# A gated two-branch decoder step: late subtractions of low parts, staged LayerNorm chunks, mixing between a pair's outputs

## The chip, the cores and the metric

One core of a Trainium2 chip runs the whole step in one program. The metric is device time in microseconds, the median of the runs; the profile is one further execution of the same program. TensorE multiplies matrices, VectorE and ScalarE work element by element, GpSimd and SyncE mostly issue transfers here.

## The reference

```python
h = rmsnorm(x, norm_g)
z = jnp.einsum('btd,de->bte', h, w_in)                 # 7 groups of 1024 columns
a_val, a_gate, a_silu, p_in, p_silu, g_a, g_b = jnp.split(z, idx, axis=-1)
u = a_val * jax.nn.sigmoid(a_gate)
c, new_conv = causal_depthwise_conv(u, buf_conv, conv_w, conv_b)      # width 31
c = jax.nn.silu(layernorm(c, ln_g, ln_b)) * jax.nn.silu(a_silu)
br_a = jnp.einsum('btc,cd->btd', c, w_conv_out)
pooled, new_pool = multiscale_pool(p_in, buf_pool, start_pos)         # means over 2, 4, 8, 16
q = jnp.einsum('btgc,gce->btge', pg, w_pool_mix).reshape(B_, T_, D_POOL)   # 4 groups of 256
q = q * pool_scale * jax.nn.silu(p_silu)
br_b = jnp.einsum('btc,cd->btd', q, w_pool_out)
merged = jax.nn.sigmoid(g_a) * br_a + jax.nn.sigmoid(g_b) * br_b
y = rmsnorm(x + jnp.einsum('btd,de->bte', merged, w_out), final_g)
```

16 learned tokens and 1024 prompt positions run with zero states, and 8 samples of 8 positions with given states. Outputs are y of both and the new states.

## The kernel before, in words

Channels lie on the 128 partitions and the 1104 positions on the free axis, in two halves h (552 each; 544 without the learned tokens, H2). A 1024-channel tensor is 8 chunks (NK). Products of fp32 precision are made from two fp32r parts: a high part (a cast on ScalarE) and a low part (source minus high part); each chunk costs three matmuls (high x high, high x low, low x high) in two column units (`gemm`, L150). The low part comes in two ways: `split` (L119) subtracts on VectorE behind the cast; `split_dma` (L124) writes minus the high part on ScalarE and adds the source by a DMA that GpSimd issues. PSUM is four buffers of two banks (`bank2`).

Order of the work: the plain outputs p0 to p5, then the plain `blocks` g0 v0 p6 p7 g1 v1 (a half output is 48 matmuls), then 22 pairs of outputs (`ORDER`: g, v, q, b, a, s). A pair makes two outputs with seven half-depth products of 24 matmuls each (`seven`, L456) out of sums of operands (`make_t`, L751, the T operands) and sums of weights (`Weights`). Products of neighbouring pairs are interleaved: q2, b, q1 of a pair, a of the next, q4, d, q3 of the next. `prepare(t)` loads a weight 8 products ahead, sums it 5 and splits it 4 ahead. Between the pairs that follow q0 to q3, `Mix` (L805) multiplies the pooled tensor by its 256 x 256 group matrices in four parts (12 matmuls each) and gates each (`gate`, L845). Then come the 8 pool outputs `ppo` (loop at L1013), the LayerNorm of the convolved tensor, the 8 conv outputs `pco` (loop at L1078, the first two made chunk by chunk in four PSUM buffers), and the last projection `pwo`.

Every engine runs its instructions in the order in which the program issues them; slots, banks and half buffers are given out in that order too (34 slots, 10 weight halves, 6 weight operands, 11 half buffers). What sets the place of VectorE's free-standing work, above all the 240 taps of the convolution (L677) and the pooling, is a planner: `todo` is a queue of (cost, work); `step(us)` advances a planned TensorE clock and runs what `defer` has put off by so many steps; `spend(n)` charges VectorE's planned clock with 0.22 + n/960 us; `fill(until)` issues work from `todo` as long as that clock is under TensorE's plus 1.5:

```python
    def fill(until=None):
        while todo and (until is None or clock["dve"] < until + LAG):
```

LayerNorm of the convolution goes over all channels, so it needs sums over the 8 chunks: `sum_rest` (L964) adds the chunks that were not stored, `begin_totals` (L970) splits the sum and defers by one step the 8 matmuls with a matrix of ones (`total_products`, L194), `centre` (L979) subtracts the mean and squares, a second `begin_totals` gives the variance, `root` (L987) the inverse root, and `branch_a` (L992) scales a chunk, applies Silu, multiplies by the silu path and splits it into the operand cx. In the `ppo` loop a step is a whole half output (6 planned us), and the fill is left out for output 0.

Of the kernel before, what the change touches and what calls it, by code (L numbers as in the profile page):

```python
# [69 lines left out]
def hybrid_trunk_kernel(  # L70
# [116 lines left out]
    def total_products(hl, n, name):  # L187
        out = slot(f"total_{name}", (2, n))
        for half in range(2):
            ps = bank2(f"pt{half}_{name}")  # L190
            for u in range(2):
                c = slice(u * n // 2, (u + 1) * n // 2)
                for i in range(2):
                    pe.matmul(ps[:, u, : n // 2], ones, hl[i][:, half, c], start=(i == 0), stop=(i == 1))  # L194
# [212 lines left out]
    class Weights:  # L407
# [19 lines left out]
        def split(self, what):  # L427
            o = op_tile(f"wo{what}_{self.name}", (2, NQ, P))
            if what in ON_DVE:
                split(o[:, 0], o[:, 1], self.raw[what])  # L430
                spend(512)
# [16 lines left out]
    def product(out, w, t, units, first, last):  # L448
        prepare(clock["t"])
        gemm(out, lambda k, s: w[:, s, k], lambda k, s: t[k][:, s], units, tuple(range(NQ)), first, last)  # L450
        clock["t"] += 1
        step(T_PRODUCT)

    def seven(w, units, put):  # L456
# [3 lines left out]
        def product_of(out, what, t, first, last):  # L460
            product(out, w.op.pop(what), t_ops[t], units, first, last)
# [16 lines left out]
        product_of(x, "q2", "T2", False, False)  # L478
        c2 = keep("c2")
# [4 lines left out]
        product_of(x, "q1", "T1", False, False)  # L484
        c4 = keep("c4")
# [319 lines left out]
    class Mix:  # L805
# [13 lines left out]
        def split_w(self):  # L819
            self.w = op_tile(f"m{self.g}", (2, 2, 2 * P))  # L820
            split(self.w[:, 0], self.w[:, 1], self.wraw.rearrange("p (k a) c -> p k (a c)", k=2))
            spend(512)
            del self.wraw

        def split(self, h):
            for k in range(2):
                self.x[k, h] = operand(f"px{2 * self.g + k}{h}", self.raw.pop((k, h)), split)
                spend(H2)
# [25 lines left out]
    for n, (kind, i) in enumerate(blocks):  # L854
        left = len(blocks) - n
        if n + 2 < len(blocks):
            ops[n + 2].load()
        if n + 1 < len(blocks):
            ops[n + 1].split(split)
            spend(512, 2)  # L860
        if left in (3, 2):
            make_t(3 - left, split_dma)
        if left == 1:
            for t in range(-LEAD_LOAD, -LEAD_SPLIT):
                prepare(t)
        for h in (0, 1) if left > 1 else (1, 0):
            ps = bank2(f"p{kind}{i}{h}")
            gemm(ps, ops[n], lambda k, s: hx[h][k][:, s], UNITS1, every, True, True)
            step(2 * T_PRODUCT)
            if kind == "v":  # L870
                fill(clock["pe"])
            put_block(kind, i, h, ps[:, :, : HT // 2])
            if left == 1:
                for t in (-4, -3) if h else (-2, -1):
                    prepare(t)
                if h:
                    make_t(2, split)
                    make_t(3, split)
            if left > 1:
                fill(clock["pe"])  # L880
        if kind == "p":
            push(pool_work(i), soon=False)
        if kind == "v":
            defer(1, lambda i=i: Conv(i))
    clock["t"] = 0
# [14 lines left out]
    mix = None  # L900
    for n in range(len(pairs)):
        nxt = pairs[n + 1][1] if n + 1 < len(pairs) else iter(())
        if mix:
            mix.split(0)
            mix.split_w()
            mix.load(1)
# [17 lines left out]
        if mix:  # L924
            mix.gate(*mix.part(1, 0))
# [4 lines left out]
        else:  # L930
            coming = None
# [28 lines left out]
    def load_sum():  # L960
        norm["sum"] = slot("lcsum", (2, H2))
        sp.dma_start(out=norm["sum"], in_=csum[0])
# [305 lines left out]
```

## Time and profile before

| | |
|---|---|
| median of 3 runs | 1029.25 us (1027.83 to 1029.61) |
| profiled execution | 1030.44 us, span 1028.7 us |
| TensorE matmul busy | 956.8 us, 93%, 7032 instructions, mean granted clock 0.964 |
| VectorE busy | 774.1 us, 75% |
| ScalarE busy | 478.6 us, 47% |
| GpSimd busy | 177.1 us, 17% |
| DMA | 187.08 MB, mean 182 GB/s |

Busy is the time in which an engine had an instruction running. A matmul counts as busy also at a low granted clock. The granted clock is a share of TensorE's 2.4 GHz; 0.5 is its lower level of 1.2 GHz. An engine that idles costs nothing unless the chain that ends last runs over it.

### The profile page before, as it was taken

To read this page: it belongs to the slowest core of one execution; us is meant where nothing else is said; L and a number is where in the kernel's file an instruction comes from. 1 tells how busy PE (TensorE), PEld (TensorE's weight loads), DVE (VectorE), ACT (ScalarE), POOL (GpSimd) and SP (SyncE) were. 2 spreads that over 40 slices of the span, in tenths; PEclk is the share of its full clock that TensorE was granted. 3 is DMA by queue.
4 is the path that set the end of the run, shared out by engine and by line. 5 is a ranking of instruction groups with operands and counts; after the bars stand their busy time and mean duration, and the time that the engine had idled before them with its cause. 6 is when DMAs were issued, how large, how long until landed. Compare 5 with 4: busy or idle time off the path is not lost.

```text
span 1028.7 us, 17986 instructions
## 1 busy us (share of the span) xinstructions
PE 956.8 (93%) x7032; PEld 930.3 (90%) x7032; DVE 774.1 (75%) x1011; ACT 478.6 (47%) x793; POOL 177.1 (17%) x216
## 2 busy tenths in 40 slices
PE   9999997999999999999999999899980779999995
PEld 9999996999999899999999999899980669998884
DVE  6569987978898878889999999669965565464343
ACT  7644345544555545555656565641145542234111
POOL 0001322322232122222232323022110100000000
PEclk9999998999999999999999999999995689999998
DMA  9323795798797876978989787997753665432222
GB/s 320 109 89 122 249 252 129 153 225 203 168 210 173 206 196 160 243 186 218 227 195 226 194 213 174 298 335 194 200 148 134 142 166 184 139 115 110 94 71 103
DMA packets 104358, 187.08 MB, mean 182 GB/s; under 512 B 21840, under 2 KB 25296, under 8 KB 104272
## 3 DMA queue, kind: packets, MB, share of 16 engines
q1 hardware_dynamic: 70720, 121.98, 37.0%
q0 software_dynamic: 24336, 46.05, 25.9%
q10 hardware_dynamic: 9216, 17.90, 4.6%
q8 instruction: 55, 0.90, 0.3%
q14 instruction: 31, 0.25, 0.1%
HBM read 93.92 MB, written 48.71 MB: 139 GB/s over the span
## 4 chain that ended last, share of the span: by engine, by line
PE 74%; DVE 11%; ACT 6%; DMA 5%; issue 3%; SPq 1%; DVEq 0%; ACTq 0%; POOLq 0%; POOL 0%
PE pp L150 9%; PE ppo L150 8%; PE pco L150 8%; PE px_b L150 5%; PE px_a L150 5%; PE pwo L1141 4%; PE px_s L150 4%; PE px_q L150 4%; PE px_v L150 4%; PE px_g L150 3%; DVE c L677 3%; PE pg L150 2%; PE pv_a L150 2%; PE pv_v L150 2%; DMA xr<-in_xres 2%
## 5 line engine op out<-in xcount | busy, mean ns | idle before, releaser
L677 DVE SCALAR_TENSOR_TENSOR c<-ce,pv,c 128x1024 f32<-128x1024 f32 x240 | 308.1, 1284 | 5.8 <-ACT c L654 1.2
L150 PE MATMUL pco<-cx,w_co 128*128 128x272 f32 x768 | 110.2, 308 | 28.3 <-ACT cx L120 14.2
L150 PEld LDWEIGHTS pco<-cx,w_co 128*128 128x128 f32 x768 | 106.9, 206 | 31.7 <-ACT cx L120 14.9
L150 PE MATMUL ppo<-q,w_po 128*128 128x272 f32 x768 | 97.0, 288 | 1.3 <-ACT w_po L120 0.9
L150 PEld LDWEIGHTS ppo<-q,w_po 128*128 128x128 f32 x768 | 96.5, 188 | 1.7 <-ACT w_po L120 1.1
L1141 PE MATMUL pwo<-wo,mx 128*128 128x512 f32 x336 | 79.2, 394 | 0.0
L1141 PEld LDWEIGHTS pwo<-wo,mx 128*128 128x128 f32 x336 | 63.1, 188 | 14.7
L150 PE MATMUL pp<-xg,wh_p 128*128 128x276 f32 x384 | 65.6, 291 | 0.4 <-DVE xg L219 0.3
L150 PEld LDWEIGHTS pp<-xg,wh_p 128*128 128x128 f32 x384 | 55.0, 189 | 1.3 <-ACT xg L218 0.7
L1160 DVE TENSOR_TENSOR xr<-pwo,xr 128x1024 f32<-128x1024 f32 (+1 forms) x9 | 10.0, 1106 | 41.2 <-PE pwo L1141 20.6
L150 PE MATMUL pp<-xg,wl_p 128*128 128x276 f32 x192 | 40.0, 290 | 0.0
L120 ACT CAST mx<-lga 128x544 fp32r<-128x544 f32 x16 | 10.3, 647 | 61.9 <-DVE lga L1102 61.9
L1123 ACT ACTIVATE sq<-xr 128x1024 f32<-128x1024 f32 (+1 forms) x9 | 8.7, 964 | 65.2 <-DVE xr L1160 65.2
L150 PE MATMUL px_q<-tT,woq_q 128*128 128x272 f32 x192 | 28.5, 310 | 4.5 <-ACT py_q L475 4.5
L150 PEld LDWEIGHTS px_q<-tT,woq_q 128*128 128x128 f32 x192 | 27.5, 210 | 4.9 <-ACT py_q L475 4.9
L125 ACT CAST w_po<-raw_po 128x512 fp32r<-128x512 f32 x14 | 8.6, 612 | 49.5 <-DMA raw_po<-in_w_po 49.1
L150 PEld LDWEIGHTS pp<-xg,wl_p 128*128 128x128 f32 x192 | 30.3, 188 | 0.0
L1101 DVE TENSOR_TENSOR lga<-pco,lga 128x544 f32<-128x544 f32 x16 | 11.6, 723 | 24.6 <-PE pco L150 24.6
L150 PE MATMUL px_b<-tT,woq_b 128*128 128x272 f32 x192 | 25.5, 289 | 2.3 <-ACT py_b L475 2.3
L150 PE MATMUL pmix<-px,m 128*128 128x272 f32 x192 | 27.1, 289 | 0.5 <-DVE zq L845 0.5
L150 PE MATMUL px_s<-tT,woq_s 128*128 128x272 f32 x192 | 25.4, 288 | 2.0 <-ACT c_s L465 2.0
L150 PEld LDWEIGHTS px_b<-tT,woq_b 128*128 128x128 f32 x192 | 24.5, 188 | 2.8 <-ACT py_b L475 2.8
(412 smaller groups left out, 2220.1 us busy)
## 6 DMA issues: line engine op xcount, KB each, us to landing
lraw<-d_raw SPq DMA_DIRECT2D x16, 276.0 KB, 3.4
d_pool<-pool SPq DMA_DIRECT2D x8, 544.0 KB, 4.5
lp<-d_pool SPq DMA_DIRECT2D x16, 272.0 KB, 4.8
lq<-d_q SPq DMA_DIRECT2D x16, 272.0 KB, 5.5
lb<-d_sgb SPq DMA_DIRECT2D x16, 272.0 KB, 4.6
d_tb<-lb SPq DMA_DIRECT2D x16, 272.0 KB, 2.5
lsa<-d_sa SPq DMA_DIRECT2D x16, 272.0 KB, 4.7
ltb<-d_tb SPq DMA_DIRECT2D x16, 272.0 KB, 3.3
```

Source lines behind the costliest of these rows:

```text
L120: act.copy(dst_h, src)
L125: act.copy(dst_h, src)
L150: pe.matmul(out[:, u, : hi - lo], w(k, a), xs(k, b)[:, lo:hi], start=first and k == ks[0] and i == 0, stop=last and k == ks[-1] and i == 2 ...
L677: dve.scalar_tensor_tensor(c, s, wk, c, ALU.mult, ALU.add)
L1101: dve.tensor_tensor(of_half(ga), ps, of_half(ga), ALU.mult)
L1123: act.activation(sq[:rows, c], xr[:, c], AF.Square, accum_out=a1 if ns[0] else a0)
L1141: pe.matmul(ps[:, n - ns[0]], x(k), wo[k][n][w], start=(k == 0 and s == 0), stop=(k == NK - 1 and s == len(passes) - 1),)
L1160: dve.tensor_tensor(v3(xr[:, c], 512), ps[:, : len(ns)], v3(xr[:, c], 512), ALU.add)
```

## The change

- `split_late` casts at once and defers the subtraction by one step. It replaces `split` for the weight q4 of each pair, for Mix's matrix and inputs, and for q chunks 0 to 5; for q 6 and 7 `split` stays and its subtractions are no longer charged to the planner.
- In `seven`, the copies c2 and c4 are issued before the step's deferred work instead of behind it, and there is one more place to pause, between product b with its output and product q1.
- Mix's part (0,0) comes before q1, its gate and part (0,1) between q1 and the next pair's a; parts (1,0) and (1,1) together between q4 and d, with their gates behind both. Its first loads are issued before the next pair's a, and its first splits behind d.
- The last two plain blocks run g1 h1, v1 h1, g1 h0, v1 h0, with `make_t(0)` to `make_t(3)` and the preparations spread between them, and fill only in v1.
- In the pool outputs a step is half a half output (3 planned us); output 0 is filled too; the stored chunks are loaded in output 0 and the sum in output 1, where the summing also enters `todo`. The mean's and variance's matmuls can so come between half products. (`begin_totals` and `total_products` take lists; each is called with one sum, as before.)
- `branch_a` is staged: the scaling and Silu of chunk i+1 are issued before chunk i's multiplication, and the subtractions of a chunk behind the next but one's scaling; its planned cost is 4.2 instead of 5.2.

```diff
+    def split_late(dst_h, dst_l, src):
+        act.copy(dst_h, src)
+        spend(src.free_size())
+        defer(1, lambda: dve.tensor_tensor(dst_l, src, dst_h.bitcast(F32), ALU.subtract))
...
-    def product(out, w, t, units, first, last):
+    def product(out, w, t, units, first, last, then):
         prepare(clock["t"])
         gemm(out, lambda k, s: w[:, s, k], lambda k, s: t[k][:, s], units, tuple(range(NQ)), first, last)
         clock["t"] += 1
+        kept = then and then()
         step(T_PRODUCT)
+        return kept
...
-        product_of(x, "q2", "T2", False, False)
-        c2 = keep("c2")
+        c2 = product_of(x, "q2", "T2", False, False, lambda: keep("c2"))
         fill(clock["pe"])
         product_of(y, "b", "21", False, True)
         fill(clock["pe"])
         put(0, 0, y[:, :, :n])
-        product_of(x, "q1", "T1", False, False)
-        c4 = keep("c4")
+        yield
+        c4 = product_of(x, "q1", "T1", False, False, lambda: keep("c4"))
...
+    ops[nb - 1].split(split)
+    spend(512, 2)
+    make_t(0, split_dma)
+    plain_half(nb - 2, 1)
+    for t in range(-LEAD_LOAD, -LEAD_SPLIT):
+        prepare(t)
+    make_t(1, split_dma)
+    plain_half(nb - 1, 1)
+    make_t(2, split)
+    prepare(-4)
+    plain_half(nb - 2, 0)
+    make_t(3, split)
+    for t in (-3, -2):
+        prepare(t)
+    plain_half(nb - 1, 0)
+    prepare(-1)
+    defer(1, lambda: Conv(blocks[-1][1]))
...
-        q.append([operand(f"q{j}{h}", z, split) for h, z in enumerate(qraw.pop(j))])
-        spend(H2, 2)
+        q.append([operand(f"q{j}{h}", z, split if j > 5 else split_late) for h, z in enumerate(qraw.pop(j))])
...
         next(cur)
         if mix:
-            mix.gate(*mix.part(0, 0))
-        next(nxt, None)
+            tail = mix.part(0, 0)
+        next(cur)
         if mix:
+            mix.gate(*tail)
             mix.gate(*mix.part(0, 1))
             mix.split(1)
-        next(cur)
-        if mix:
-            mix.gate(*mix.part(1, 0))
         if 0 <= n - first_q < 4:
             coming = Mix(n - first_q)
             coming.load(0)
             coming.load_w()
-        else:
-            coming = None
+        next(nxt, None)
+        next(cur)
+        if mix:
+            tails = [mix.part(1, 0), mix.part(1, 1)]
+            for tail in tails:
+                mix.gate(*tail)
...
         next(cur)
-        tail = mix.part(1, 1) if mix else None
+        if coming:
+            coming.split(0)
+            coming.split_w()
+            coming.load(1)
         next(nxt, None)
-        if tail:
-            mix.gate(*tail)
         next(nxt, None)
-        mix = coming
+        mix, coming = coming, None
...
+    def scale(i):
+        if i < NK:
+            dve.tensor_tensor(conv[i], conv[i], norm["rstd"], ALU.mult)
+            act.activation(conv[i], conv[i], AF.Silu, bias=col(OFF_LB, i), scale=col(OFF_LG, i))
...
     def branch_a(i):
+        scale(i + 1)
+        while low:
+            low.popleft()()
+        if i == NK:
+            return
         load_sa(i + 2)
         cx.append([])
...
-            cx[i].append(operand(f"cx{i}{h}", conv[i][:, h], split_dma if i in (1, 3, 5) else split))
+            if i in (1, 3, 5):
+                cx[i].append(operand(f"cx{i}{h}", src, split_dma))
+            else:
+                o = slot(f"cx{i}{h}", (2, H2), F32R)
+                act.copy(o[:, 0], src)
+                low.append(
+                    lambda o=o, src=src: dve.tensor_tensor(o[:, 1], src, o[:, 0].bitcast(F32), ALU.subtract)
+                )
+                cx[i].append(o)
...
-            ps = gemm_half(f"ppo{d}", po[d], q, h, NK)
-            step(2 * T_PRODUCT)
-            if d < 2:
-                load_conv(d * 4 + h * 2, d * 4 + h * 2 + 2)
-            if d == 2 and h == 0:
+            ps = bank2(f"ppo{d}{h}")
+            for ks in (range(NQ), range(NQ, NK)):
+                gemm(ps, po[d], lambda k, s: q[k][h][:, s], UNITS3, tuple(ks), ks[0] == 0, ks[0] > 0)
+                step(T_PRODUCT)
+                if ks[0] == 0 and d > 0:
+                    fill(clock["pe"])
+            ps = ps[:, :, : H2 // 2]
+            if d == 0:
+                load_conv(h * 4, h * 4 + 4)
+            if d == 1 and h == 0:
                 load_sum()
...
-            if d > 0:
-                fill(clock["pe"])
+            fill(clock["pe"])
```

## Rows read from the trace of the kernel before

**Rows 1.** Page, the chain that ended last, shares of the span by engine

```profile
PE 74%; DVE 11%; ACT 6%; DMA 5%; issue 3%; SPq 1%; DVEq 0%; ACTq 0%; POOLq 0%; POOL 0%
```

**Rows 2.** Windows: from:to, length, busy per engine (instructions), TensorE's clock, DMA share, GB/s

```profile
153.60:176.60 23.00, 15.76 (x98) 14.77 (x98) 18.41 (x25) 12.56 (x22) 4.88 (x6) 0.78 0.59 128
...
326.00:446.00 120.00, 112.69 (x864) 111.36 (x864) 102.43 (x126) 59.40 (x100) 25.79 (x30) 0.97 0.76 197
446.00:650.00 204.00, 204.00 (x1632) 204.00 (x1631) 186.78 (x208) 120.65 (x198) 59.54 (x74) 1.00 0.85 207
650.00:671.40 21.40, 16.59 (x127) 15.73 (x125) 16.20 (x24) 14.82 (x26) 0.86 (x1) 1.00 0.99 314
...
768.60:797.50 28.90, 2.55 (x8) 1.92 (x8) 17.55 (x17) 14.87 (x15) 0.00 (x0) 0.59 0.45 141
797.50:847.70 50.20, 36.10 (x192) 33.24 (x192) 29.88 (x38) 23.86 (x33) 5.19 (x6) 0.76 0.60 151
```

**Rows 3.** Timeline, first pair: start, us, engine, line, what [idle before <- releaser]

```profile
162.08 2.65 DVE L121 TENSOR_TENSOR tT<-ts,tT 128x552 fp32r<-128x552 f32 x4
...
168.51 5.30 PE L150 MATMUL px_g<-tT,woq_g 128*128 128x276 f32 x24 [4.36 <-ACT py_g L475]
```

**Rows 4.** Timeline, two of the four mixes

```profile
330.07 3.16 PE L150 MATMUL px_q<-hx,woa_q 128*128 128x272 f32 x24
...
332.86 0.78 DVE L845 SCALAR_TENSOR_TENSOR zq<-pmix,pv,zq 128x544 f32<-128x544 f32 x1
...
342.47 6.56 DVE L677 SCALAR_TENSOR_TENSOR c<-ce,pv,c 128x1024 f32<-128x1024 f32 x5
...
348.95 0.78 DVE L845 SCALAR_TENSOR_TENSOR c_q<-pmix,pv,c_q 128x544 f32<-128x544 f32 x1
...
350.42 4.81 PE L150 MATMUL px_q<-tT,woq_q 128*128 128x272 f32 x24 [2.51 <-ACT py_q L475]
...
362.77 0.79 DVE L845 SCALAR_TENSOR_TENSOR zq<-pmix,pv,zq 128x544 f32<-128x544 f32 x1 [2.84 <-PE pmix L150]
```

**Rows 5.** Timeline, last pair

```profile
657.64 0.61 ACT L465 COPY c_s<-px_s 128x544 f32<-128x544 f32 x1 [2.29 <-DMA d_sa<-c_s]
...
658.31 3.25 PE L150 MATMUL px_s<-tT,woq_s 128*128 128x272 f32 x24 [2.03 <-ACT c_s L465]
```

**Rows 6.** Timeline, VectorE in the pool outputs

```profile
677.27 0.72 DVE L1029 TENSOR_TENSOR lb<-ppo,lb 128x544 f32<-128x544 f32 x1 [4.65 <-PE ppo L150]
...
757.17 3.69 DVE L981 TENSOR_TENSOR lc<-lc,total_mean 128x1088 f32<-128x1088 f32 x3 [6.94 <-ACT total_mean L195]
```

**Rows 7.** Timeline, LayerNorm's chunks on VectorE and ScalarE

```profile
793.45 1.29 DVE L995 TENSOR_TENSOR lc<-lc,ir_c 128x1088 f32<-128x1088 f32 x1
794.78 1.29 ACT L996 ACTIVATE lc<-lc,pv 128x1088 f32<-128x1088 f32 x1 [3.47 <-DVE lc L995]
796.10 0.73 DVE L998 TENSOR_TENSOR lc<-lc,lsa 128x544 f32<-128x544 f32 x1 [1.36 <-ACT lc L996]
...
797.54 0.72 DVE L121 TENSOR_TENSOR cx<-lc,cx 128x544 fp32r<-128x544 f32 x1 [0.71 <-ACT cx L120]
...
803.66 0.65 ACT L125 CAST cx<-lc 128x544 fp32r<-128x544 f32 x1 [0.80 <-DVE lc L998]
...
811.58 1.28 DVE L995 TENSOR_TENSOR lc<-lc,ir_c 128x1088 f32<-128x1088 f32 x1
```

**Rows 8.** Timeline, from the first conv output to the third

```profile
842.17 0.72 DVE L1101 TENSOR_TENSOR lga<-pco,lga 128x544 f32<-128x544 f32 x1 [1.02 <-PE pco L150]
...
847.74 74.21 PE L150 MATMUL pco<-cx,w_co 128*128 128x272 f32 x576 [3.35 <-ACT w_co L120]
```

**Rows 9.** SyncE: one issue; waits (total, times, longest); one load (KB, us to landing)

```profile
338.61 2.81 SPq L790 DMA_DIRECT2D lp<-d_pool  x2
...
SPq L790 <- DVE lc L998: 39.7, 11, 14.2
...
a_q<-in_w_in SPq DMA_DIRECT2D x4, 256.0 KB, 4.5
```

More of the change, by code (lines that the diff above doesn't have):

```diff
@@ L192, in total_products @@
                 c = slice(u * n // 2, (u + 1) * n // 2)
-                for i in range(2):
-                    pe.matmul(ps[:, u, : n // 2], ones, hl[i][:, half, c], start=(i == 0), stop=(i == 1))
+                for i, part in enumerate(hl):
+                    pe.matmul(
+                        ps[:, u, : n // 2], ones, part[:, half, c], start=(i == 0), stop=(i == len(hl) - 1)
+                    )
             act.copy(v3(out[:, half], n // 2), ps[:, :, : n // 2])
@@ L429, in split @@
             if what in ON_DVE:
-                split(o[:, 0], o[:, 1], self.raw[what])
-                spend(512)
+                split_late(o[:, 0], o[:, 1], self.raw[what])
             else:
@@ L458, in seven, with product_of @@
         name = w.name
-        def product_of(out, what, t, first, last):
-            product(out, w.op.pop(what), t_ops[t], units, first, last)
+        def product_of(out, what, t, first, last, then=None):
+            return product(out, w.op.pop(what), t_ops[t], units, first, last, then)
         def keep(what):
@@ L826, in split @@
             for k in range(2):
-                self.x[k, h] = operand(f"px{2 * self.g + k}{h}", self.raw.pop((k, h)), split)
-                spend(H2)
+                self.x[k, h] = operand(f"px{2 * self.g + k}{h}", self.raw.pop((k, h)), split_late)
         def part(self, h, i):
@@ L853, in hybrid_trunk_kernel, with plain_half @@
         push(pool_work(j))
[L854 to L868, printed above, removed]
-            step(2 * T_PRODUCT)
-            if kind == "v":
-                fill(clock["pe"])
[L872 to L880, printed above, removed]
+    def plain_half(n, h):
+        kind, i = blocks[n]
+        ps = bank2(f"p{kind}{i}{h}")
+        gemm(ps, ops[n], lambda k, s: hx[h][k][:, s], UNITS1, every, True, True)
+        step(2 * T_PRODUCT)
+        if kind == "v":
+            fill(clock["pe"])
+        put_block(kind, i, h, ps[:, :, : HT // 2])
+    nb = len(blocks)
+    for n, (kind, i) in enumerate(blocks[:-2]):
+        ops[n + 2].load()
+        ops[n + 1].split(split)
+        spend(512, 2)
+        for h in (0, 1):
+            plain_half(n, h)
+            fill(clock["pe"])
         if kind == "p":
@@ L899, in hybrid_trunk_kernel @@
     after = iter(())
-    mix = None
+    mix = coming = None
     for n in range(len(pairs)):
         nxt = pairs[n + 1][1] if n + 1 < len(pairs) else iter(())
-        if mix:
-            mix.split(0)
-            mix.split_w()
-            mix.load(1)
         if n + 1 == len(pairs):
@@ L962, in load_sum @@
         sp.dma_start(out=norm["sum"], in_=csum[0])
+        push(summing)
     def sum_rest(i):
@@ L967, in sum_rest, with begin_totals @@
             dve.tensor_tensor(norm["sum"], norm["sum"], conv[i], ALU.add)
-    def begin_totals(key, name, work):
-        parts_ = total_parts(norm[key], H2, name)
+    def begin_totals(keys, name, work):
+        more = [total_parts(norm[key], H2, f"{name}{n}") for n, key in enumerate(keys)]
         def run():
-            norm[name] = total_products(parts_, H2, name)
+            norm[name] = total_products([t for hl in more for t in hl], H2, name)
             push(work)
@@ L1017, in hybrid_trunk_kernel @@
         for h in range(2):
[L1018 to L1022 removed]
+            ps = bank2(f"ppo{d}{h}")
[3 more added lines that the diff above has]
+                if ks[0] == 0 and d > 0:
+                    fill(clock["pe"])
+            ps = ps[:, :, : H2 // 2]
+            if d == 0:
+                load_conv(h * 4, h * 4 + 4)
+            if d == 1 and h == 0:
                 load_sum()
@@ L1025, in hybrid_trunk_kernel @@
                 co[1].split(split_dma)
-            if d > 0:
-                fill(clock["pe"])
+            fill(clock["pe"])
             z = lb[d][h]
```

21 lines of the change are left out of this document (11 added, 10 removed).

## The prediction

> **What bounds the kernel now.** I read the chain of waits first: TensorE carries 74% of it, VectorE 11%, ScalarE 6%, transfers 5% [rows 1]. So the time is TensorE's own work plus the places where it stands or runs slowly; VectorE is a second, nearly full engine beside it. The stage windows say where those places are [rows 2]. In 446 to 650 us TensorE is busy throughout: 1632 matmuls of 272 columns in 204 us, 0.125 us each at a granted clock of 1.00. I count the other stages in that unit (0.127 for the 276 columns of the first ones); what a stage takes beyond it is lost:
> - A, first pair (153.6 to 176.6): 98 matmuls need 12.4 of 23.0 us, 10.6 lost.
> - B, the four mixes (326 to 446): 864 need 108 of 120, 12.0 lost.
> - C, last pair and the casts of q (650 to 671.4): 127 need 15.9 of 21.4, 5.5 lost.
> - D, between the pool outputs and the first conv output (768.6 to 797.5): 8 matmuls in 28.9, 27.9 lost.
> - E, the first two conv outputs (797.5 to 847.7): 192 need 24.0 of 50.2, 26.2 lost, 3.4 of it at the very end.
> Together 82 us; the change touches exactly these five. Nothing outside them can give much.
>
> **The change part by part**, against the profiled execution's own 1030.4 us (span 1028.7 and 1.7 around it); the median of the runs is 1029.25, 1.2 below it, and I take that off at the end.
>
> *A: blocks g1, v1 in the order h1, h1, h0, h0, and make_t spread between them.* Today make_t(2) and make_t(3) run inside the first pair: their last four subtractions end at 164.7, and TensorE stands 4.36 us for the copy of the first output, which sits on ScalarE behind their casts and those of the next weights; then 24 matmuls take 5.30 us, slow clock included [rows 3]. After it make_t(2) is issued when v1's half 1 ends and make_t(3) one half product (48 matmuls, 6.0 us) later, two and one half products before the pair, where today both start in the last one. The four subtractions take 2.65 us [rows 3], a make_t is eight such instructions, 5.3; both and three sums fit into the 12 us. Moved against it: v1's weights are wanted 6 us earlier, and the taps not filled during g1 come in one burst before v1's output. What is left is the last summed weight of T2, which I put at 2 us. Gain 8.6; bounds 4 (the burst holds the subtractions and sums back by about a make_t) and 10.6.
>
> *B: mixing between a pair's outputs.* Today the gate of the fourth mix matmul is queued behind five taps (6.56 us), ends at 349.7, only then is its PSUM bank free for y, ScalarE copies, and TensorE has stood 2.51 us; the next 24 matmuls take 4.81 instead of 3.0 [rows 4]. After it both gates of the second half stand directly behind their matmuls, with d's product (3.0 us) before anyone wants their banks, and the copies c2 and c4 go before deferred casts. So this stall goes. What is late next: part(0,0) moves before q1, its gate stays behind q1's fill, and the next pair's product a needs that bank after only part(0,1), 12 matmuls, 1.5 us. The fill runs VectorE at least 1.5 us past TensorE, the gate takes 0.78: 0.8 us of standing. The trace has both ends: a gate 2.76 us behind its matmul's end at 330.1 (ending 3.5 behind, so 2.0 of standing), and one for which VectorE was early and waited 2.84 itself (none) [rows 4]. I take 1.2 for each of four, 5 in all: gain 7. Bounds 12 (none) and -5 (the rival below). split_late here only takes VectorE's waits for casts away; the deferred subtractions are wanted two products later.
>
> *C: split_q late, keep before step.* The copy c_s stood behind four casts of q, themselves behind loads of q; TensorE stood 2.03 us, with the 24 matmuls then at 3.25, so no slow clock [rows 5]. keep is now issued before what step() runs, so the copy comes first. The 16 casts and 16 subtractions remain, and so does the wait for po's first weight, since the transfers are full there (share 0.99) [rows 2]; I leave 2 us for these: gain 3.5, bounds 0 and 5.5.
>
> *D: sums between half products, fill in the first pool output.* VectorE idles 4.65 us in the first half of pool output 0, and about as long in the second, since nothing is filled there [rows 6]; now taps are. That time alone moves nothing, since the planner fixes behind which matmuls the sums come; it lets VectorE, today those 9 us behind, keep to the plan. What moves the sums is the grid: steps of 3 us instead of 6, and 4 subtractions of q (j > 5) no longer charged, 4 x 0.787 = 3.15 us of planned work. Counting the planner's costs through the remaining taps and sums, begin_totals comes out half way through the 13th of 16 half products instead of behind it, and the products of the mean at the end of the 13th instead of the 14th: one half product, 6.0 us. The squares are bound by VectorE (15 x 1.28 and three outputs of 0.72, some 21.4 us) and start 6 us earlier, so the variance, root and all behind it do too. Gain 6.0; bounds 3 (a quarter) and 9 (the mean's wait of 6.94 us in [rows 6] and a quarter more). Loading the chunks two half products earlier adds 1.1 MB to 671 to 684, wanted 60 us later: nothing.
>
> *E: chunks in stages.* Today each chunk runs multiply, Silu, multiply, cast, subtract as one chain over two engines: three chunks from 793.45 to 811.58, 6.04 us each [rows 7]. After it the next chunk's multiply and Silu and the last one's subtraction fill those waits. VectorE then has 8 x 1.28, 16 x 0.73 and 10 x 0.72 = 29.1 us, ScalarE 8 x 1.29 and 22 casts or negations of 0.65 = 24.6 [rows 7]: VectorE bounds, 3.6 us a chunk. Laying the instructions out by hand, the first low part is ready 6.1 us after the start (4.8 today), and the last half-0 one at 30.2. 6 matmuls at up to 0.2 us later the first output is complete (31.5), and from there to the next weights it is what it is today: VectorE's first merge at 842.17 to 847.74, and 0.3 before it, 5.9 us [rows 8]. That is 37.4 us against 847.74 - 793.45 = 54.3: gain 16.9. Bounds 19 (the merge chain's 3.35 us hidden in part) and 0.5 (next paragraph).
>
> TensorE's clock in that stretch: it runs at 0.59 of full before and 0.76 in E [rows 2], so it comes back slow and recovers in part. At half speed throughout, 192 matmuls take 48 us, from 4.6 to 52.6 after the start, and with it E gives about 0.5. The Trainium skill (TensorE: Matmul & The Clock Gate, section "HAM oscillation — how this bites in real kernels") says that short bursts of matmuls with operand waits between them start cold every time; by that rule E would stay near those 48 us. The granted 0.76 with the waits of today lies half way; after the change a chunk brings 3.0 us of matmuls each 3.6 us, so I take the recovery.
>
> Sum: 8.6 + 7 + 3.5 + 6.0 + 16.9 = 42.0. 1030.4 - 42.0 = 988.4, on the scale of the runs 987.
>
> **The rivals.**
> 1. *The slow clock holds through E.* For it: 0.76 and 0.59 in the windows. Against: 24 matmuls in 4.81 us, not 6.0, after the stall in B [rows 4], so the clock returns within one product. E gives 0.5 instead of 16.9: 1003.
> 2. *The bank wait in B is as long as the stall removed.* 2.0 us of standing and 1.8 of slow clock, four times, and one more microsecond at d: about 17 lost instead of 12. For it the 2.76 us lag; against it VectorE's own 2.84 us of waiting. 987 + 12 = 999.
> 3. *VectorE becomes the bound*: TensorE's gains in A to C (19.1) are given back in D because the taps are not done. VectorE is busy 92% in 446 to 650 [rows 2] and would have to do the same before the mean in 25 us less. Only D and E stay: 1006.
> 4. *Slower: SyncE stands on Mix's loads.* coming.load(0) now goes before a and q4, with the 11 half buffers nearly all held by gates, copies and the other half's inputs. Weights loaded 8 products ahead and cast 4 ahead have 12 us, less 4.5 of landing [rows 9]: 7.5 of slack. Slower from 18 us of standing a pair on (4 x (18 - 7.5) = 42); at the 21 us that a whole pair takes it is 4 x 13.5 = 54 us and 1041. Today such a load took 2.81 us and the longest SyncE wait for a half buffer is 14.2 [rows 9], within what still gains.
>
> That the change doesn't do what it says: the waits only move to the next engine in each of the five places, and the time stays at 1029.
>
> **How the numbers follow.** Forecast 987: 0.60, its own range 975 to 998 (A, B and C together 10 to 25, E 13 to 19). Rival 1: 0.13, rival 2: 0.10, rival 3: 0.08, no change 0.04, rival 4: 0.05. About 0.2% is what runs of this kernel can tell from no change. Faster is forecast and rivals 1 to 3, 0.91; same 0.04; slower 0.05. The range reaches over rivals 1 to 3 to 1008; at the other end all upper bounds together give 56 and 973, of which I keep 972: outside lie rival 4 and no change, 0.09 (at 1029 and above), and about 0.1 of sums beyond its two ends.
>
> **What would show it.** A: the products of the first pair follow each other within 2 us in all, clock 1.00. B: no standing at y, instead under 1.5 us before product a of the pair after each of q0 to q3. C: no wait of px_s for c_s. D: no idle VectorE in the first pool output, the mean's products one half product earlier, TensorE standing about 22 us before the first conv output instead of 29. E: multiplies 3.6 us apart, and 37 us from the first to the third output's products. Wrong if D stands as long as before, if E's granted clock stays near 0.6, or if SyncE's loads of lp are late.

## The result, and the profile after

The changed kernel takes 997.2 us (median of runs; 996.5 to 999.4), the kernel before 1029.4 beside it: ratio 0.9687, 95% interval 0.966 to 0.9714. So it is faster by 32 us, where 42 were forecast; the time lies near the upper end of the forecast's own range (975 to 998), and 10 us above the value.

The page of the changed kernel: busy time, and the shares of the chain that ended last (answers to [rows 1]).

```profile
PE 947.1 (95%) x7032; PEld 923.5 (93%) x7032; DVE 771.1 (77%) x1011; ACT 477.4 (48%) x793; POOL 174.3 (18%) x216
...
PE 76%; DVE 10%; DMA 6%; ACT 5%; issue 3%; SPq 1%; ACTq 0%; DVEq 0%
```

TensorE's share of the chain rises from 74 to 76%, that of the transfers from 5 to 6, VectorE's falls from 11 to 10: the path still consists of TensorE's own work, with less standing in between.

Its windows over the same five stages, first pair to conv outputs (columns as in [rows 2], of which they are the answer):

```profile
154.10:173.40 19.30, 14.54 (x99) 13.77 (x98) 19.05 (x24) 11.63 (x21) 5.86 (x7) 0.91 0.69 139
326.00:440.00 114.00, 113.51 (x902) 112.90 (x901) 104.56 (x123) 62.60 (x104) 25.26 (x31) 1.00 0.84 219
640.00:657.50 17.50, 12.68 (x98) 12.03 (x96) 11.52 (x18) 12.59 (x23) 0.78 (x1) 1.00 0.96 322
755.90:777.00 21.10, 2.55 (x10) 1.82 (x8) 11.49 (x12) 12.57 (x13) 0.00 (x0) 0.60 0.46 159
777.00:815.00 38.00, 30.45 (x192) 29.25 (x192) 26.48 (x36) 21.54 (x31) 5.19 (x6) 0.81 0.74 201
```

In the prediction's unit (0.127 us a matmul in the first stage, 0.125 in the others, 8 matmuls for D) the lost time is: A 19.3 - 99 x 0.127 = 6.7 (10.6 before), B 114 - 902 x 0.125 = 1.2 (12.0), C 17.5 - 98 x 0.125 = 5.2 (5.5), D 21.1 - 1.0 = 20.1 (27.9), E 38.0 - 24.0 = 14.0 (26.2). That is 47 us instead of 82, and 35.0 gained; the spans differ by 1028.7 - 995.5 = 33.2, since some matmuls at a low clock lie just outside the windows. The expectations below count each stage by how much earlier the same product starts, which includes those matmuls: A 3.3, B 10.1, C -1.0, D 8.1, E 12.1 (E from the first conv output's start to the third's; from the first scaling on, as the prediction counts, it is 54.3 - 42.4 = 11.9).

### The profile page after: what moved, and what is told of

Its sections match the earlier page's. It is cut to its first block, busy times and chain, and to the rows that moved or that the text cites. A ratio compares the mean times of both kernels' runs of the same rounds, so it can differ in the third digit from the quotient of the medians.

```text
span 995.5 us, 18002 instructions
## 1 busy us (share of the span) xinstructions
PE 947.1 (95%) x7032; PEld 923.5 (93%) x7032; DVE 771.1 (77%) x1011; ACT 477.4 (48%) x793; POOL 174.3 (18%) x216
## 4 chain that ended last, share of the span: by engine, by line
PE 76%; DVE 10%; DMA 6%; ACT 5%; issue 3%; SPq 1%; ACTq 0%; DVEq 0%
PE ppo L156 10%; PE pco L156 9%; PE pp L156 7%; PE px_a L156 5%; PE pwo L1181 4%; PE px_q L156 4%; PE px_b L156 4%; PE px_s L156 4%; PE px_v L156 4%; PE px_g L156 3%; PE pv_b L156 2%; PE pv_a L156 2%; PE pv_s L156 2%; PE pv_v L156 2%; PE pv_q L156 2%
## 5 line engine op out<-in xcount | busy, mean ns | idle before, releaser
L156 PE MATMUL pco<-cx,w_co 128*128 128x272 f32 x768 | 104.2, 300 | 22.1 <-ACT cx L1030 14.5
L156 PEld LDWEIGHTS pco<-cx,w_co 128*128 128x128 f32 x768 | 102.8, 199 | 23.6 <-ACT cx L1030 14.8
L1141 DVE TENSOR_TENSOR lga<-pco,lga 128x544 f32<-128x544 f32 x16 | 11.6, 722 | 31.6 <-PE pco L156 31.6
L133 POOL DMA_DIRECT2D w_po<-raw_po x14 | 12.2, 868 | 78.0 <-DMA d_sa<-c_s 22.0
L156 PE MATMUL px_q<-tT,woq_q 128*128 128x272 f32 x192 | 25.5, 288 | 0.0
L156 PE MATMUL px_a<-tT,woq_a 128*128 128x272 f32 x192 | 25.4, 288 | 0.0
L156 PE MATMUL pg<-hx,w_g 128*128 128x276 f32 x192 | 24.9, 290 | 0.0
```

The costliest lines, as they stand in the source:

```text
L156: pe.matmul(out[:, u, : hi - lo], w(k, a), xs(k, b)[:, lo:hi], start=first and k == ks[0] and i == 0, stop=last and k == ks[-1] and i == 2 ...
L1141: dve.tensor_tensor(of_half(ga), ps, of_half(ga), ALU.mult)
```

## Experiments: each part undone by itself

Each run here is the changed kernel with one part set back; what that costs is what the part gave. Spans are those of the one profiled execution, to be set against 995.5; ratios are to the kernel before, to be set against 0.9687. Runs of one kernel lie up to 4.5 us apart, so the ratio alone tells only B and E from nothing; A and D are read from positions in the trace.

| undone | median, us | ratio, 95% interval | span | costs (span) | forecast | by windows |
|---|---|---|---|---|---|---|
| A: order of the last blocks | 1001.2 | 0.971 (0.9694-0.9727) | 998.5 | 3.0 | 8.6 | 3.9 |
| B: order of the mixing | 1003.0 | 0.9736 (0.9719-0.9753) | 1004.1 | 8.6 | 7 | 10.8 |
| C: late subtractions, early copies | 996.9 | 0.9674 (0.9653-0.9695) | 994.6 | -0.9 | 3.5 | 0.3 |
| D, its grid: sums between half products | 999.0 | 0.9692 (0.9678-0.9707) | 998.8 | 3.3 | 6.0 with the next | 7.8 with the next |
| D, its charge: q 6 and 7 not counted | 1002.1 | 0.9722 (0.9699-0.9745) | 999.7 | 4.2 | | |
| E: chunks in stages | 1008.0 | 0.9778 (0.9761-0.9795) | 1006.1 | 10.6 | 16.9 | 12.2 |

The six spans add up to 28.8 of 33.2 us.

**A undone** (the make_t, prepares and blocks as before):

```diff
-    make_t(1, split_dma)
-    plain_half(nb - 1, 1)
-    make_t(2, split)
...
+        if left in (3, 2):
+            make_t(3 - left, split_dma)
...
+                if h:
+                    make_t(2, split)
+                    make_t(3, split)
```

> Part A alone undone: the last two blocks of the first pair in the old order, the T transforms, casts and prepares where they stood before. Theory 1 (stage by stage, from how much earlier the same product starts in the changed kernel): A is worth 3.3 us, because the waits that went (4.36 before px_g) came back as 3.11 on the load of woa_g and 1.10 on woq_g; so 997.2 + 3.3 = 1000.5 us. Theory 2 (the prediction's term): 8.6 us, so about 1005.8. If a later stage absorbs what A gives, 997.

1001.2 us, span + 3.0: theory 1. The timeline of the changed kernel around its first pair shows where the other 5 us of the forecast went (against [rows 3]):

```profile
147.12 1.28 DVE L685 SCALAR_TENSOR_TENSOR c<-ce,pv,c 128x1024 f32<-128x1024 f32 x1 [5.59 <-ACT c L662]
148.32 0.73 DVE L726 TENSOR_TENSOR zg<-pv,zg 128x552 f32<-128x552 f32 x1
148.96 0.72 DVE L762 TENSOR_TENSOR ts<-x,x 128x552 f32<-128x552 f32 x1
...
152.85 0.62 ACT L131 CAST woa_g<-a_g 128x512 fp32r<-128x512 f32 x1
...
157.88 3.93 PE L156 MATMUL px_g<-hx,woa_g 128*128 128x276 f32 x20 [3.11 <-DMA woa_g<-a_g]
...
163.83 2.80 PE L156 MATMUL pv_g<-tT,woq_g 128*128 128x276 f32 x20 [1.10 <-DMA woq_g<-q_g]
...
167.18 3.31 PE L156 MATMUL px_g<-tT,woq_g 128*128 128x276 f32 x24 [0.55 <-ACT py_g L484]
```

VectorE's first tap stands 5.59 us for a copy that ScalarE makes only behind the casts and negations of make_t(0) and (1); the gate and make_t(2) stand behind that tap. The 4.36 us in front of px_g are 0.55 now, but the weights' casts came late, and their low parts cost 3.11 and 1.10 us.

**B undone** (gates and first loads as before, the splits before the pair):

```diff
-            mix.gate(*tail)
             mix.gate(*mix.part(0, 1))
...
-            tails = [mix.part(1, 0), mix.part(1, 1)]
-            for tail in tails:
-                mix.gate(*tail)
...
+        tail = mix.part(1, 1) if mix else None
         next(nxt, None)
+        if tail:
+            mix.gate(*tail)
```

> Part B alone undone: the gates of the mixing products and the casts of the next one's operands stand again where they stood before among a pair's outputs; kept casts and late subtractions stay. Theory 1 (stage by stage): the waits in the mixes come back, 12.0 us of them before against 1.9 after, so +10.1: 1007.3 us. Theory 2 (the prediction's term): +7: 1004.2. Rival 2 of the prediction (the earlier mixing product puts a bank wait before the next pair's product) would make undoing it worth nothing or less: 997 or below.

1003.0 us and + 8.6 in the span; the runs themselves say 5 to 6, nearer theory 2, since the profiled execution was the slowest of the four, 2.9 us above their median. TensorE's timeline in the mixes, first the changed kernel, then with B undone (against [rows 4]):

```profile
328.65 3.27 PE L156 MATMUL px_q<-hx,woa_q 128*128 128x272 f32 x24 [0.23 <-DVE zq L851]
...
343.90 3.28 PE L156 MATMUL px_q<-tT,woq_q 128*128 128x272 f32 x24
```

```profile
345.69 4.80 PE L156 MATMUL px_q<-tT,woq_q 128*128 128x272 f32 x24 [1.88 <-ACT py_q L484]
...
376.50 4.79 PE L156 MATMUL px_q<-tT,woq_q 128*128 128x272 f32 x24 [1.94 <-ACT py_q L484]
```

The waits for the copy of y are back, 1.88, 1.94, 0.54 and 1.76 us in the four mixes, and after two of them 24 matmuls take 4.8 us instead of 3.2: 6.1 + 3.2 = 9.3. The bank wait of rival 2 is 0.23 us at one pair, 0.26 at another and none at two.

**C undone** (subtraction at once, copies behind the step):

```diff
     def split_late(dst_h, dst_l, src):
-        act.copy(dst_h, src)
+        split(dst_h, dst_l, src)
         spend(src.free_size())
-        defer(1, lambda: dve.tensor_tensor(dst_l, src, dst_h.bitcast(F32), ALU.subtract))
...
-        kept = then and then()
         step(T_PRODUCT)
-        return kept
+        return then and then()
```

> Late subtractions and early copies undone together (part C, and the same edit in the weights and in the mixes): each subtraction is issued behind its cast again, c2 and c4 behind the step's deferred work. Theory 1 (the four single undos A, B, D, E cost 3.0, 8.6, 3.3 and 10.6 us in their profiled spans, 25.5 of the 33.2 between before and after; the rest, 7.7, is this edit and the planner's charge for the last subtractions of q, of which this kernel undoes the first): 4 to 5 us, 1001 to 1002 us. Theory 2 (the prediction's term C): 3.5 us, 1000.7. Theory 3 (stage by stage C gives nothing, the wait on c_s is only replaced by the one on w_po): 997.

996.9 us: nothing, theory 3. Timelines of the last pair, first the changed kernel, then with C undone (against [rows 5]):

```profile
646.35 3.27 PE L156 MATMUL px_s<-hx,woq_s 128*128 128x272 f32 x24 [0.70 <-ACT c_s L474]
...
651.37 1.28 ACT L125 CAST q<-lq 128x544 fp32r<-128x544 f32 x2 [3.98 <-DMA lq<-d_q]
...
655.76 1.14 ACT L120 CAST w_po<-raw_po 128x512 fp32r<-128x512 f32 x2
...
656.43 0.77 PE L156 MATMUL ppo<-q,w_po 128*128 128x272 f32 x4 [3.81 <-ACT w_po L120]
```

```profile
644.67 0.61 ACT L472 COPY c_s<-px_s 128x544 f32<-128x544 f32 x1 [2.10 <-DMA d_sa<-c_s]
...
645.34 4.80 PE L155 MATMUL px_s<-tT,woq_s 128*128 128x272 f32 x24 [1.82 <-ACT c_s L472]
...
658.03 0.77 PE L155 MATMUL ppo<-q,w_po 128*128 128x272 f32 x4 [0.93 <-ACT w_po L120]
```

The first wait for c_s (1.82 us, and 1.6 us of slow matmuls behind it) does go with the change; the second copy's, 0.70 us, stays. But TensorE then only comes earlier to po's weight, whose cast ScalarE makes behind those of q, which stand for a load (3.98 us): 3.81 us instead of 0.93. With C undone ScalarE itself idles 2.10 us in front of the copy, until the store d_sa<-c_s lands (644.59, the copy starts at 644.67); the 2.29 us in [rows 5] are the same wait. So what released the copy was a half buffer coming free, not the end of the casts of q. In the changed kernel the copy no longer waits for one, and SyncE's loads of q stand for such a store twice (6.2 us from 634 to 650) instead of once (4.6). One run more, with that cast ahead of q's last ones:

```diff
-            defer(5, lambda: po[0].split(split))
+            defer(4, lambda: po[0].split(split))
```

> The cast of the last projection's first weight one product sooner in ScalarE's order (deferred 4 products instead of 5), ahead of the last casts of q. Theory 1 (the 3.81 us that the first projection waits for w_po are lost, and 1 to 2 us more by the slow clock behind them): 3.5 to 5 us less, 992 to 993.7 us. Theory 2 (ScalarE has no room: the casts of q then come late and the score products wait instead): 0 us or up to 2 us more, 997 to 999.

997.9 us (ratio 0.968, 0.9667 to 0.9694): nothing again. TensorE's timeline in that kernel:

```profile
652.77 4.51 PE L156 MATMUL ppo<-q,w_po 128*128 128x272 f32 x32 [0.35 <-ACT w_po L120]
658.54 8.79 PE L156 MATMUL ppo<-q,w_po 128*128 128x272 f32 x68 [1.27 <-DVE q L127]
670.33 19.96 PE L156 MATMUL ppo<-q,w_po 128*128 128x272 f32 x145 [2.99 <-DMA w_po<-raw_po]
```

The output starts 3.6 us earlier and stands for the last q and for po's second weight, which lands at 670 us. Started at 652.8, 656.4 or 658.0, the outputs end at 756.9, 756.1 and 756.2. Theory 2 has the size, and half of the cause: the pool outputs (its "score products") do wait for q, 1.27 us, but longer for a weight that has not landed.

**D, grid undone** (with it the filling of output 0 and the earlier loads of the chunks and the sum, not shown):

```diff
-            for ks in (range(NQ), range(NQ, NK)):
-                gemm(ps, po[d], lambda k, s: q[k][h][:, s], UNITS3, tuple(ks), ks[0] == 0, ks[0] > 0)
-                step(T_PRODUCT)
...
+            ps = gemm_half(f"ppo{d}", po[d], q, h, NK)
+            step(2 * T_PRODUCT)
```

> Part D alone undone: whole products of the last projection between two turns of the LayerNorm sums. Theory 1 (stage by stage): the mean comes 1.5 half products later and the stretch from it to the first convolution output grows, together 8.1 us: 1005.3 us. Theory 2 (the prediction's term): 6.0 us: 1003.2. If VectorE, busy 9.8 tenths in that stretch in the changed kernel, sets the mean anyway: 997 to 999.

**D, charge undone** (the same instructions, another plan):

```diff
         q.append([operand(f"q{j}{h}", z, split if j > 5 else split_late) for h, z in enumerate(qraw.pop(j))])
+        if j > 5:
+            spend(H2, 2)
```

> Only the charge put back: the planner's VectorE clock counts the subtractions of q 6 and 7 again (4 x 0.787 us of planned work); every instruction is the same, only the order behind it can move. Theory 1 (that charge is what part D has beside its finer grid: with the grid undone alone the mean's products come 3.6 us later, against 7.5 between before and after, measured from the first pool output): the mean's products come at the next half product's half, 3 us later, 1000 us. Theory 2 (the remaining 3.9 us come from the late subtractions, not from the charge): 0 us, 997.

The grid alone cost 3.3 us in the span (0.5 by the ratios, which can't tell it from nothing), below both theories; the charge 4.2, 1002.1 us (its ratio's interval still overlaps the changed kernel's), theory 1 in effect though not in size: the products of the mean came 6 us later, not 3. TensorE's timeline: changed, grid undone, charge undone (the first pool output starts at 656.4, 656.2 and 656.2).

```profile
733.87 0.29 PE L200 MATMUL pt_mean<-sumh_mean,ones 128*128 128x272 f32 x1
...
759.25 0.39 PE L200 MATMUL pt_var<-sumh_var,ones 128*128 128x272 f32 x1 [3.15 <-ACT sumh_var L120]
...
777.02 0.82 PE L156 MATMUL pco<-cx,w_co 128*128 128x272 f32 x2 [14.49 <-ACT cx L1030]
```

```profile
737.45 0.29 PE L200 MATMUL pt_mean<-sumh_mean,ones 128*128 128x272 f32 x1
...
762.67 0.59 PE L200 MATMUL pt_var<-sumh_var,ones 128*128 128x272 f32 x1 [6.02 <-ACT sumh_var L120]
```

```profile
739.72 0.29 PE L200 MATMUL pt_mean<-sumh_mean,ones 128*128 128x272 f32 x1
...
763.06 0.60 PE L200 MATMUL pt_var<-sumh_var,ones 128*128 128x272 f32 x1 [7.13 <-ACT sumh_var L120]
...
780.83 0.82 PE L156 MATMUL pco<-cx,w_co 128*128 128x272 f32 x2 [14.49 <-ACT cx L1032]
```

The later the mean, the longer TensorE stands for the sum of the variance; behind it the 14.49 us to the first chunk are the same. So by these traces about half of D's gain is the finer grid, with the filling and loads undone beside it, and half a number in the planner's account.

**E undone** (scaling, cast and subtraction of a chunk in one piece, at the planned cost of 5.2 again):

```diff
     def branch_a(i):
-        scale(i + 1)
-        while low:
-            low.popleft()()
...
+        scale(i)
...
-                act.copy(o[:, 0], src)
-                low.append(
...
+                cx[i].append(operand(f"cx{i}{h}", src, split))
```

> Part E alone undone: each chunk's scaling, cast and subtraction again in one piece, chunk after chunk, instead of the scaling one chunk ahead and the subtraction one chunk behind. Theory 1 (stage by stage): from the first scaling to the third output 54.3 us before, 42.4 after, so 12.1 us: 1009.3 us. Theory 2 (the prediction's term): 16.9 us: 1014.1. Rival 1 of the prediction (TensorE's slow clock makes the stretch as long either way): 0.5 us, 997.7.

1008.0 us, span + 10.6: theory 1, and the no-gain rival is out. From the first scaling to the start of the last matmul of the conv outputs it is 115.9 us in the changed kernel, 127.9 here and 128.2 before, so nearly all of E's gain is this edit.

## Experiments: what bounds the first conv outputs now

The changed kernel's timeline from the first scaling on (against [rows 7, 8]):

```profile
772.61 2.49 DVE L1010 TENSOR_TENSOR lc<-lc,ir_c 128x1088 f32<-128x1088 f32 x2
...
781.56 0.86 POOL L133 DMA_DIRECT2D cx<-lc  x1 [30.76 <-DVE lc L1010]
782.78 0.86 POOL L133 DMA_DIRECT2D cx<-lc  x1 [0.36 <-ACT cx L132]
...
786.08 1.02 PE L156 MATMUL pco<-cx,w_co 128*128 128x272 f32 x6 [1.92 <-DMA cx<-lc]
788.70 22.99 PE L156 MATMUL pco<-cx,w_co 128*128 128x272 f32 x160 [1.61 <-DMA cx<-lc]
...
799.70 1.36 DVE L1032 TENSOR_TENSOR cx<-c,cx 128x544 fp32r<-128x544 f32 x2
809.48 0.72 DVE L1141 TENSOR_TENSOR lga<-pco,lga 128x544 f32<-128x544 f32 x1 [8.42 <-PE pco L156]
...
815.05 7.21 PE L156 MATMUL pco<-cx,w_co 128*128 128x272 f32 x45 [3.36 <-ACT w_co L120]
```

VectorE is done with the chunks at 801.06, 28.5 us after the start, and then idles 8.42 us for TensorE. TensorE has 160 of its 192 matmuls left at 788.70, when the second of chunk 1's low parts has come, a transfer issued at 782.78; it needs 22.99 us for them, some 3 more than at 0.125 us each. (A merge, L1141, is VectorE's first step on a finished conv output.)

**A higher clock in front of the first conv outputs** (128 matmuls that nothing reads, 24 and 104, while TensorE waits):

```diff
+    keep_warm(WARM_VAR, "warmv")
     while todo or due:
         fill()
         step(0.0)
+    keep_warm(WARM_CO, "warmc")
```

> The changed kernel and 128 matmuls more on TensorE whose result nothing reads (24 before the variance products, 104 before the first convolution outputs), in the time in which it waits for the LayerNorm statistics and the first scaled chunk. Nothing is left out. Theory 1 (TensorE's clock sets the stretch of the early outputs: granted 0.50, 0.67 and 0.80 from 770 to 800, VectorE done with the chunks 8 us before the merges): the early outputs run at full clock, the stretch is then as long as VectorE's chunks, about 8 us less: 989 us. Theory 2 (the operands of the chunks, VectorE and ScalarE, set the stretch): 0 us, 997. If the added matmuls delay the sums or the first output: above 997.

995.2 us (ratio 0.9666, 0.9651 to 0.9681), not told from the changed kernel. Windows of both, the changed one first:

```profile
770.00:780.00 10.00, 2.31 (x8) 1.99 (x9) 9.74 (x12) 5.52 (x7) 0.00 (x0) 0.50 0.18 56
...
790.00:800.00 10.00, 10.00 (x67) 10.00 (x67) 8.48 (x13) 7.99 (x12) 1.77 (x3) 0.80 1.04 255
```

```profile
770.00:780.00 10.00, 7.67 (x48) 7.23 (x47) 9.80 (x12) 6.94 (x9) 0.39 (x1) 0.83 0.30 89
...
790.00:800.00 10.00, 10.00 (x82) 10.00 (x81) 7.68 (x11) 6.30 (x10) 1.72 (x2) 1.00 1.04 272
```

The granted clock rose there, and from the first scaling to the first merge 36.9 us became 36.0. The 8 us of theory 1 did not come, but the clock was not taken away as a cause. Behind the wait for chunk 1's second transfer it is at its lower level in both kernels; a window of the changed one, then a window and TensorE's line of the one with the unread matmuls:

```profile
789.00:791.00 2.00, 2.00 (x10) 2.00 (x10) 1.91 (x3) 2.00 (x4) 0.87 (x1) 0.50 0.93 197
```

```profile
787.00:789.00 2.00, 2.00 (x11) 2.00 (x10) 1.91 (x3) 2.00 (x3) 0.87 (x1) 0.50 0.92 190
...
786.47 13.78 PE L157 MATMUL pco<-cx,w_co 128*128 128x272 f32 x96 [1.33 <-DMA cx<-lc]
```

What slow matmuls cost there is read from the starts of the 160: above 0.125 us each they lose 2.7 us in the changed kernel and 1.7 with the unread matmuls (each without a short stand for chunk 5's transfer, 0.38 us in the second). What ran before them, slow or not, had to wait for chunk 1's transfers. So up to the first merge the clock is worth at most 2.7 us here, not 8. The Trainium skill (TensorE: Matmul & The Clock Gate, section "HAM oscillation — how this bites in real kernels") has bursts with operand waits between them start cold. The trace agrees in part: the matmuls behind the waits of 1.61 and 1.33 us ran at 0.50 at first, while with the unread matmuls 6 behind a wait of 2.94 us took 1.02 us, which is the full clock.

**The third output's weight ahead of the merges:**

```diff
-        if 0 < d < NK - 1:
+        if 1 < d < NK - 1:
             co[d + 1].split(split)
...
                     gemm(ps, co[d_], lambda k, s: cx[k][h][:, s], UNITS3, (k,), k == 0, k == NK - 1)
+            co[2].split(split)
```

> The cast of the third convolution output's weight put ahead of the merges of the first two outputs in the order of ScalarE and VectorE. Theory 1 (TensorE's wait of 3.36 us for w_co and the slow clock behind it, 29 matmuls in 5.20 us, are lost time): 4 to 5 us less, 992 to 993 us. Theory 2 (the merges come later by as much as the cast comes sooner, and the tail waits for them): 0 us, 997.

991.9 us (ratio 0.9628, 0.9614 to 0.9642): theory 1 by the runs; in the traces it is 3.0 us of this stretch, and 3.9 of the span. No wait for w_co is left; instead TensorE stands once for chunk 5's transfer:

```profile
802.97 27.25 PE L156 MATMUL pco<-cx,w_co 128*128 128x272 f32 x203 [1.85 <-DMA cx<-lc]
```

**Chunk 5's low part on VectorE as well**, without and with the unread matmuls:

```diff
-            if i in (1, 3, 5):
+            if i in (1, 3):
                 cx[i].append(operand(f"cx{i}{h}", src, split_dma))
```

> The earlier cast of the third output's weight, and chunk 5's low part made by VectorE instead of by a transfer, so that no operand of chunk 5 comes over the queue whose share is 1.04 from 790 to 800. Theory 1 (with the earlier cast TensorE waits 1.85 us for chunk 5's transfer at 803, and VectorE has 6 us left behind its last chunk): 1.8 us below the 991.9 of the earlier cast alone, about 990 us. Theory 2 (VectorE bounds the chunks: 1.36 us more on it delay chunks 6 and 7 as much): 992 to 993 us.

> The same with the 128 matmuls that nothing reads (24 before the variance products, 104 before the first convolution outputs). Theory 1 (two limits lie one behind the other: alone, the full clock gave 0.8 us in this stretch because TensorE then ran into the transfer of chunk 5; with that transfer gone it gives all): 2 to 3 us below the kernel without them, about 987.5 us. Theory 2 (the clock costs nothing in this stretch, whatever the operands): the same as the kernel without them, 990 us.

991.5 us (0.9614, 0.959 to 0.9637) and 990.1 (0.9609, 0.9588 to 0.963); both intervals overlap that of the earlier cast alone. From the first scaling to the start of the last matmul of the conv outputs it is 113.0 us with the earlier cast, 110.6 with chunk 5 on VectorE, 109.6 with the unread matmuls too: the transfer is worth 2.4 us there, a little above theory 1, and the unread matmuls 1.0, less than the 2 to 3 expected; the clock is at 0.50 again from 785 to 791. The first of the two lies between its theories by the runs. The second is the fastest measured, faster than the kernel before and the changed one. Its timeline says what binds it:

```profile
785.46 1.73 PE L157 MATMUL pco<-cx,w_co 128*128 128x272 f32 x6 [2.79 <-DMA cx<-lc]
787.58 42.61 PE L157 MATMUL pco<-cx,w_co 128*128 128x272 f32 x324 [0.40 <-DMA cx<-lc]
...
807.43 0.72 DVE L1151 TENSOR_TENSOR lga<-pco,lga 128x544 f32<-128x544 f32 x1 [5.28 <-PE pco L157]
```

Its scaling starts at 771.96; chunk 1's transfers are in 15.6 us later. The first merge needs 142 of the 160 matmuls that are then left (the last 18 belong to the other three half outputs): 17.8 us at 0.125 each and 1.9 of slow clock, together 35.3; it comes at 35.5. Chunk 1 without transfers was not run.

**A tap less in front of the third transform** (part A):

```diff
-        if kind == "v":
+        if kind == "v" and not late:
             fill(clock["pe"])
...
-    plain_half(nb - 1, 1)
+    plain_half(nb - 1, 1, True)
```

> One deferred convolution's turn not taken between the last v block's product and its gate, so that VectorE's gate and third T transform are not queued behind a tap which waits 5.59 us for a copy of ScalarE that stands behind 16 casts. Theory 1 (that tap is what part A lost): the third T transform starts some 6 us sooner, woa_g's cast and load with it, and the 3.11 and 1.10 us of waits on these loads go: 4 to 5 us less, 992 to 993 us. Theory 2 (the loads wait for the weight's own place in the order, not for VectorE): 0 us, 997.

997.4 us (0.9679, 0.9666 to 0.9693): nothing, though half of theory 1 came true. TensorE's timeline:

```profile
164.13 3.33 PE L156 MATMUL px_g<-tT,woq_g 128*128 128x276 f32 x24 [1.68 <-ACT py_g L484]
...
181.98 4.84 PE L156 MATMUL pv_g<-tT,wod_g 128*128 128x276 f32 x24 [2.33 <-DVE c_g L497]
```

The wait for woa_g fell from 3.11 to 0.76 us and the pair's product came 3.05 us earlier; then VectorE's sum c_g (L497), queued behind the taps that had been put off, held TensorE 2.33 us, and 24 matmuls behind it took 1.6 us longer. In the changed kernel VectorE is busy 19.05 of the 19.30 us of stage A, where it was busy 18.41 of 23.00 before [rows 2]. That fits a stage which VectorE now bounds; less work for VectorE there was not run.

## Why the prediction came out as it did

That the time lies in the forecast's own range is in part luck: B and D gave 5.6 us more than their terms, A, C and E 12.6 less. With B and D as forecast it would have been about 1003 (997.2 + 5.6), outside it.

**A, 8.6 forecast, 3 to 4 found,** under its lower bound of 4. The mechanism held, the step "What is left is the last summed weight of T2, which I put at 2 us" was mis-sized. It counted VectorE's work into the 12 us, but not that its first tap waits for ScalarE behind the 16 casts and negations of the transforms moved there; what is left are 3.11, 1.10 and 0.55 us of waits and the matmuls slowed behind them. With that tap put off the loss only moved on (997.4 us), so what bounds A now stays open in part.

**B, 7 forecast, 8.6 to 10.8 found in the traces, 5 to 6 in the medians.** Right. The 1.2 us of bank wait were 0.23 and 0.26 where there were any: rival 2 fell. Nor did SyncE's loads hold anything up (rival 4).

**C, 3.5 forecast, nothing found.** The prediction reads the copy as standing "behind four casts of q, themselves behind loads of q"; [rows 5] names the store d_sa<-c_s, which kept the copy's half buffer. The failed step is "I leave 2 us for these: gain 3.5". The wait for po's first weight is not a remainder but the next wait of the chain, 3.81 us and 1.5 us of slow matmuls (11 in 2.86 us), and behind it comes po's second weight. The lower bound, 0, was the true one, and the sentence that gave it (the transfers are full there) points at the reason: loads of q and of po's weights that land late. That fewer transfers there would make C pay was not tried.

**D, 6.0 forecast, 7.8 found.** Right in mechanism: the mean comes 12.5 half products after the start instead of 14 (13 was forecast), the standing fell from 27.9 to 20.1 us. Both halves of the argument, the grid and the uncharged subtractions, were needed; undone singly they cost 3.3 and 4.2 us.

**E, 16.9 forecast, 11.9 found.** VectorE's account was right (28.5 us for the chunks, 29.1 forecast). The failed step is "6 matmuls at up to 0.2 us later the first output is complete (31.5)": TensorE does not walk behind VectorE but has 160 of its 192 matmuls left 16.1 us after the first scaling, because both low parts of chunk 1 are transfers. They landed about 4.5 and 5.9 us after their issue, a term the sum did not have. From there 142 matmuls at 0.125 us (17.8) and 2.7 us of slow clock make 36.6; the first merge came at 36.9 instead of 31.8, and from it to the third output it took 5.6 us, as predicted. The trace of the kernel before had this wait already, three times (3.88, 2.13 and 3.27 us):

```profile
808.76 1.73 PE L150 MATMUL pco<-cx,w_co 128*128 128x272 f32 x6 [3.88 <-DMA cx<-lc]
```

The Trainium skill (DMA: Bandwidth & Descriptors, section "Anatomy of one DMA — SWDGE (gpsimd) path") fits a transfer on this path as 2.0 us and its bytes at 436 GB/s, which gives an estimate of 2.6 us for 272 KB; the traces show 3.3 and 4.1 us for chunk 1 before and 4.5 and 5.9 after, and the traces decide.

Rival 1 named the slow clock, and the clock was low (0.50, 0.67, 0.80); its price of 16 us was wrong, since the slow matmuls that could delay the first output cost 2.7. Rival 3 (VectorE becomes the bound) fits A at most: its time of 1006 did not come, because A to C's gains were not given back before the mean. The sum of the misses, A - 4.7, B + 3.8, C - 3.2, D + 1.8, E - 4.7, by the windows, is - 7.0: 35.0 where 42 stood.

## What to carry to other kernels

When a wait is removed, price the next arrival at the same place before booking the gain: list when each further operand lands, and whether it comes by a transfer; here the stretch that compute had made shorter ended at its first late transfer. An engine's busy share in the new, shorter stage, work moved in over time left, can be worked out in advance; in A it came to 99% for VectorE, and the gain stayed at less than half of the forecast. When an experiment is to take a cause away, look whether it is gone at the place where it acts: the unread matmuls raised the clock in front of the stretch, and it was low again behind the next wait. A planner's cost entries are part of a kernel's schedule: a single charge of 3 us of planned work moved the end of the profiled execution by 4 us with no instruction changed.

## What the runs showed of the hardware

A transfer that adds into its destination, 272 KB, took 4.5 to 7.8 us from issue to landing (median 5.5) in the changed kernel, beside a DMA share of 0.9 to 1.04; the same six took 3.3 to 4.8 (median 4.0) before, where they lay further apart. Four of 256 KB took 7.9 to 8.9 us (median 8.5) where the share was 1.0. In ten kernels with the same instructions up to there, the waits for woa_g's and woq_g's transfers were 1.5 to 3.2 and 1.1 to 2.6 us: differences below 2 us between single executions are of that size. With B undone, a wait of 1.9 us in the mixes was followed by 24 matmuls in 4.8 us at one place and, after 1.76 us, by 24 in 3.28 at another; in the last pair 24 took 4.80 us behind 1.82 with C undone, and 3.25 behind 2.03 before [rows 5]. What decides is not shown by these runs.
